# Attention maxima with a pace of their own, retention steps shifted by one, and the second half's head sums taken early

## The chip, the cores and the metric

The kernel runs on one core of a Trainium2 chip. Five engines work side by side, each on its own queue in program order: TensorE (PE: matmuls and transposes, its weight loads shown apart as PEld), VectorE (DVE), ScalarE (ACT), GpSimd (POOL) and SyncE (SP), which here only issues DMAs. The metric is the device time of one execution in microseconds. Before the change it is 2969.17 us, the median of three runs (2965.57 to 2970.82).

## The reference, cut to what matters

A decoder block over 2048 tokens of width 1024, all in float32:

```python
h = rms_norm(x, attn_norm_w)
r_q, r_k, r_v, r_g, c_q, c_kv, k_pe = split(h @ w_in)
y_ret = retention_group(r_q, r_k, r_v, r_g, ...)  # 8 heads of 64: causal scores with decay,
                                                  # a state carried over chunks, group norm, silu gate
y_mla = mla_group(c_q, c_kv, k_pe, ...)           # 8 heads: causal softmax attention, low-rank q and kv
x = x + concat(y_ret, y_mla) @ w_out
x = x + conv_ffn(rms_norm(x, ffn_norm_w))         # 1024 -> 2*2816, causal conv of width 3, silu gate, -> 1024
return rms_norm(x, final_norm_w)
```

The causal softmax is `p = softmax(where(key <= query, s, -big))`. The row maximum that is taken off before the exponential must see the masked scores; any shift that is the same for a row gives the same result.

## The kernel before

Matmul operands that carry float32 are split into a high part (rounded copy) and a low part (the difference): `split` (L60 to L68) makes the high part on ACT (L64) or DVE and the low part on POOL or DVE (L68), and `mm3` (L72 to L74) issues three matmuls per product. So nearly every matmul waits for an ACT copy and a POOL or DVE subtraction, and a product is ready only when its low part is.

The program runs in stages. First the input projections that attention needs. Then `side_by_side` runs two generators against each other: `ret_stream` (retention, 16 chunk pairs of 256 tokens for two pairs of heads) and `att_stream` (attention, 8 heads of 4 groups of 512 queries). Each generator yields the cost of the step that it has just written, and the order of the instructions follows from these costs. The compiler's scheduler then fixes each engine's order from the written order and the waits.

A retention chunk (`ret_chunk`) has 16 steps: eight projection steps, and eight that split q and k (tile S), transpose S on PE (L619), form and mask the scores (tile x), multiply with V, update the state, and norm and gate (L682 to L693). The last eight run beside the eight projection steps of the next chunk, one to one. An attention group (`att_group`) has 4g+5 steps: scores (PE, tile s; L759 to L764), exponentials on ACT and their low parts on DVE (tile pc, L768), and the products with v (tile o). Before a group can start, `att_max` must have found the row maxima of its queries: for each of the 4 blocks of 128 queries and each chunk of 512 keys one score matmul into the PSUM tile sm (L727), for the chunk on the diagonal a second matmul that adds the mask (L730: identity `unit` times `mqk`, 256 columns), and a reduction on DVE (L731). sm has one buffer, so the next L727 waits for the L731 before it. The maxima of the next group are spread over the steps of the current one: 4g'+6 units over 4g+5 steps.

Then `out_stream` puts the first eight tokens' tiles (128 tokens each) through the output projection, and `half_0_forms` adds the retention part of the output projection for tiles 8 to 15 (the transposes of the token forms are at L955) and prepares the first half's up-projection operands F (low parts: POOL, L68). `up` (L1087 on) is the up-projection of a half with its conv (L1135 to L1138) and gate; `down` the down-projection and the final norm. Between the halves `half_1_forms` adds the attention heads' part of the output projection for tiles 8 to 15: `att_load` brings the two halves of a head sum (mixa_s) and the softmax denominators' reciprocals (rden_s), POOL adds and scales them (L851, L852), the operands are split, PE multiplies, DVE adds to the residual (L868), ACT squares (L1039), DVE takes the root in ten small instructions (L102 to L114) and scales (L1042), and PE transposes the result for the up-projection.

Of the kernel before, what the change touches and what calls it, by code (L numbers as in the profile page):

```python
# [46 lines left out]
AHEAD = 2  # L47
RET_SHARE = .91
# [5 lines left out]
class Block:  # L54
# [388 lines left out]
    def att_pools(self, ctx):  # L443
        nc, a, tc = self.nc, self.a, self.tc
        self.kp = ctx.enter_context(tc.tile_pool(name="ak", bufs=5, side="right"))
# [8 lines left out]
        m = b1.tile([P, 640], F32R, name="mqk")  # L454
        r = self.raw.tile([P, D], F32, name="raw")[:, :640]
        nc.sync.dma_start(r, a["mask_att"])
        nc.scalar.activation(m, r, AF.Copy)
        self.mkq, self.mqk = m[:, 0:384], m[:, 256:640]
# [3 lines left out]
        self.vts = [b1.tile([P, 4, 160], F32R, name=f"v{i}") for i in range(5)]  # L462
# [54 lines left out]
    def ret_stream(self):  # L517
        nc, a = self.nc, self.a
        hs, pend = {}, None
# [29 lines left out]
        for c in pend:  # L549
            yield c  # L550

    def att_stream(self):
        groups = [(h, g) for h in range(H) for g in range(4)]
        q = None
        for c, q in self.att_max(*groups[0]):
            yield c
        for n, (h, g) in enumerate(groups):
            nxt = self.att_max(*groups[n + 1]) if n + 1 < len(groups) else iter(())
            steps, units = 4 * g + 5, 4 * groups[n + 1][1] + 6 if n + 1 < len(groups) else 0
            owed, qn = 0.0, None  # L560
            for c in self.att_group(h, g, q):
                owed += units / steps
                while owed >= 1:
                    owed -= 1
                    m = next(nxt, None)
                    if m:
                        c += m[0]
                        qn = m[1]
                yield c
            for m in nxt:  # L570
                qn = m[1]
                yield m[0]
            q = qn
# [3 lines left out]
    def ret_chunk(self, p, ch, W, hs):  # L577
        nc, c1, c2, px = self.nc, self.r1, self.r2, self.pr_x
        mm = nc.tensor.matmul
        qk = c2.tile([P, 2, 4, 64], F32, name="qk")  # L580
        vg = c2.tile([P, 2, 256], F32, name="vg")
        V = c2.tile([P, 2, 2, 2, 64], F32R, name="V")
        sg = c2.tile([P, 2, P], F32, name="sg")
# [64 lines left out]
        o = c2.tile([P, 4, 64], F32, name="o")  # L648
# [32 lines left out]
        sq = c1.tile([P, 4, 64], F32, name="gsq")  # L681
# [31 lines left out]
    def att_max(self, h, g):  # L713

        nc, b2 = self.nc, self.b2
        q = b2.tile([98, 2, 512], F32R, name="q")
# [3 lines left out]
        mx = b2.tile([P, 4, 4], F32, name="mx")  # L720
        for i in range(4):
            for c in range(g + 1):
# [4 lines left out]
                nc.tensor.matmul(ps[:, :N], lhsT=q[0:96, 0, i * P:(i + 1) * P], rhs=k[0:96, 0, :N], start=True, stop=c < g)  # L727
# [116 lines left out]
    def att_load(self, t, r, rd, m):  # L844

# [5 lines left out]
        nc.gpsimd.tensor_tensor(r[:, 0], r[:, 0], r[:, 1], op=ALU.add)  # L851
        nc.gpsimd.tensor_tensor(r[:, 0], r[:, 0], rd, op=ALU.mult)  # L852
# [124 lines left out]
    def half_0_forms(self):  # L977
# [3 lines left out]
        def rows(i):  # L981
            for j in range(2):
                nc.sync.dma_start(hn[2 * (i % 2) + j], self.hn_s[4 * j + i])
        for t in (8, 9):
            self.z0_load(t)
        rows(0)
        rows(1)
        for i in range(4):
            self.token_forms(i, hn[2 * (i % 2)], hn[2 * (i % 2) + 1])
# [4 lines left out]
            for t in (8 + 2 * i, 9 + 2 * i):  # L994
                m, y = self.ms[t % 2].rearrange("p (a k x) -> p a k x", a=2, k=4), self.ys[t % 2]
                pss = [self.bank() for _ in range(2)]
                for kc in range(4):
                    self.out_mm(pss, m, kc, kc == 0, kc == 3)
                self.out_add(y, pss)
                nc.sync.dma_start(self.y_s[t], y)  # L1000
                if t + 2 < NT:
                    self.z0_load(t + 2)
# [7 lines left out]
    def z1_load(self, n, r=None):  # L1010
        t = Z1_ORDER[n]
        r = (self.raws[n % 2] if r is None else r).rearrange("p (a k x) -> p a k x", a=2, k=4)
        self.att_load(t, r, self.p1.rearrange("p (k x) -> p k x", k=4), self.ms[n % 2].rearrange("p (a k x) -> p a k x", a=2, k=4))

    def z1_early(self, n):

        if n == 2 * NFB - 3:
            self.nc.sync.dma_start(self.u2.rearrange("p a b -> p (a b)"), self.a["ffn_norm_w"].broadcast_to([P, D]))
            self.ms = self.slots(1)
        if n >= 2 * NFB - 2:  # L1020
            k = n - (2 * NFB - 2)
            self.z1_load(k, self.u.rearrange("p a b -> p (a b)")[:, k * D:(k + 1) * D])

    def half_1_forms(self):

        nc, hn, fnw = self.nc, self.fs, self.u2.rearrange("p a b -> p (a b)")
        for n in range(2):
            nc.sync.dma_start(self.ys[n], self.y_s[Z1_ORDER[n]])
        self.pay()
# [368 lines left out]
```

## Time and profile before

| | before |
|---|---|
| median of 3 runs | 2969.17 us |
| profiled execution | 2968.21 us (span 2966.4 us, 1.8 us around it) |
| PE busy | 2768.4 us (93%) |
| DVE busy | 1953.1 us (66%) |
| ACT busy | 1348.3 us (45%) |
| POOL busy | 1957.8 us (66%) |
| retention and attention side by side | 270 to 1290 us |
| half_0_forms | 1423 to 1484 us |
| up, down of the first half | 1484 to 1922, 1922 to 2179 us |
| half_1_forms | 2179 to 2282 us |
| up, down of the second half | 2282 to 2700, 2700 to 2966 us |

Busy time of PE is modelled (matmuls are pipelined, their durations overlap), so the step from the start of one to the start of the next counts, and so do the idle times before an instruction together with what ended them. PEclk is the clock that was granted to TensorE, as a share of its upper level, 2.4 GHz; 0.5 is the lower one, 1.2 GHz.

### The profile page before, as it was taken

The page shows a single profiled execution, that of the slowest core. Times are in us where ns is not written, and L with a number is a line of the kernel's source. Part 1 is how long each engine was busy: PE and PEld are TensorE (multiplying, and loading weights), DVE is VectorE, ACT ScalarE, POOL GpSimd, SP SyncE. Part 2 cuts the span into 40 slices and gives each one's busy share as a digit, 9 for nine tenths or more (in the row PEclk, how much of TensorE's full clock was granted, in tenths as well). Part 3 has the DMA queues.
Part 4 walks back from the last instruction along what each step waited for, and adds up shares of the span by engine and source line. Part 5 has one row for each costly group of instructions (what it writes and reads, how often), then busy time and mean ns, then how long its engine had stood idle before and what let it go on. Part 6 is the DMA issues. An engine that isn't in the chain of part 4 may idle for free.

```text
span 2966.4 us, 37611 instructions
## 1 busy us (share of the span) xinstructions
PE 2768.4 (93%) x12800; PEld 2237.1 (75%) x12800; DVE 1953.1 (66%) x3265; ACT 1348.3 (45%) x2544; POOL 1957.8 (66%) x1478
## 2 busy tenths in 40 slices
PE   7998999988999999989899999989995999999998
PEld 6976777777777777767787777778874888887887
DVE  8765676667666666754458888844266888887243
ACT  5435656555655555551333333333334433333343
POOL 2035656566655556663599999765558999995564
PEclk9999999999999999999899999989997999999999
DMA  7663112223211121326622222264552222224453
GB/s 259 219 209 95 53 55 65 59 70 97 63 54 55 54 65 45 97 88 196 241 94 77 73 85 81 79 228 153 187 192 96 71 79 86 79 74 163 149 193 109
DMA packets 153360, 332.91 MB, mean 112 GB/s; under 512 B 35016, under 2 KB 68296, under 8 KB 147024
## 3 DMA queue, kind: packets, MB, share of 16 engines
q1 hardware_dynamic: 153168, 330.51, 34.1%
q8 instruction: 101, 1.65, 0.2%
q14 instruction: 91, 0.75, 0.1%
HBM read 237.71 MB, written 92.75 MB: 111 GB/s over the span
## 4 chain that ended last, share of the span: by engine, by line
PE 56%; DVE 15%; ACT 7%; issue 6%; POOL 6%; DMA 3%; SPq 0%; POOLq 0%; ACTq 0%; DVEq 0%
PE b L74 10%; PE b L73 10%; PE b L72 10%; PE pm L74 3%; PE pm L72 3%; PE pm L73 3%; DVE w L1137 2%; DVE u L1131 2%; DVE w L1138 2%; PE sm L727 2%; ACT w L1136 2%; PE s L759 2%; PE x L661 2%; DVE w L1163 2%; PE s L764 1%
## 5 line engine op out<-in xcount | busy, mean ns | idle before, releaser
L68 POOL TENSOR_TENSOR w<-raw,w 128x512 fp32r<-128x512 f32 (+2 forms) x315 | 523.2, 1676 | 256.2 <-ACT w L64 243.8
L74 PE MATMUL b<-F,w 128*128 128x512 f32 x1232 | 492.5, 400 | 0.0
L72 PE MATMUL b<-F,w 128*128 128x512 f32 x1232 | 487.7, 396 | 3.8 <-DVE u L1131 3.8
L73 PE MATMUL b<-F,w 128*128 128x512 f32 x1232 | 487.5, 396 | 3.1 <-POOL F L68 3.1
L777 POOL TENSOR_TENSOR den<-den,pc 128x512 f32<-128x512 f32 (+2 forms) x256 | 294.1, 1149 | 207.8 <-ACT pc L766 189.8
L64 ACT ACTIVATE w<-raw 128x512 fp32r<-128x512 f32 (+2 forms) x328 | 214.4, 658 | 348.1 <-PE b L74 179.0
L72 PE MATMUL b<-w 128*128 128x512 f32 x832 | 330.2, 397 | 21.0 <-DVE u L1131 13.0
L74 PE MATMUL b<-w 128*128 128x512 f32 x832 | 328.1, 394 | 1.6 <-POOL w L68 1.5
L73 PE MATMUL b<-w 128*128 128x512 f32 x832 | 328.0, 394 | 0.0
L731 DVE TENSOR_REDUCE mx<-sm 128x1 f32<-128x512 f32 (+2 forms) x320 | 194.1, 607 | 173.8 <-PE sm L727 126.9
L68 DVE TENSOR_TENSOR w<-xr,w 128x512 fp32r<-128x512 f32 x88 | 110.4, 1255 | 284.9 <-ACT w L64 284.9
L72 PEld LDWEIGHTS b<-F,w 128*128 128x128 f32 x1232 | 232.6, 189 | 65.7 <-DVE u L1131 11.0
L73 PEld LDWEIGHTS b<-F,w 128*128 128x128 f32 x1232 | 232.5, 189 | 62.4 <-POOL F L68 3.5
L74 PEld LDWEIGHTS b<-F,w 128*128 128x128 f32 x1232 | 232.4, 189 | 54.5
L768 DVE TENSOR_TENSOR pc<-s,pc 128x512 fp32r<-128x512 f32 (+1 forms) x320 | 197.6, 619 | 99.6 <-ACT s L767 74.6
L1136 ACT ACTIVATE w<-u,cw 128x1024 f32<-128x1024 f32 x88 | 109.5, 1244 | 333.1 <-DVE u L1131 198.5
L1137 DVE SCALAR_TENSOR_TENSOR w<-u,cw,w 128x1024 f32<-128x1024 f32 x88 | 165.7, 1883 | 128.7 <-ACT w L1136 128.7
L766 ACT ACTIVATE pc<-s 128x512 fp32r<-128x512 f32 (+1 forms) x320 | 172.6, 539 | 148.5 <-PE s L764 142.1
L72 PE MATMUL pm<-w,h 128*128 128x512 f32 x512 | 211.1, 412 | 6.3 <-DVE t L598 4.8
L68 POOL TENSOR_TENSOR w<-xr,w 128x512 fp32r<-128x512 f32 x110 | 204.6, 1872 | 9.4 <-ACT w L64 9.4
L74 PE MATMUL pm<-w,h 128*128 128x512 f32 x512 | 206.5, 403 | 0.0
L73 PE MATMUL pm<-w,h 128*128 128x512 f32 x512 | 205.7, 402 | 0.0
(263 smaller groups left out, 6618.6 us busy)
## 6 DMA issues: line engine op xcount, KB each, us to landing
raw<-in_w_down SPq DMA_DIRECT2D x88, 512.0 KB
h<-hT_s SPq DMA_DIRECT2D x32, 1024.0 KB
xr<-in_w_up SPq DMA_DIRECT2D x44, 512.0 KB
raw<-in_w_up SPq DMA_DIRECT2D x44, 512.0 KB
g_s<-w SPq DMA_DIRECT2D x44, 512.0 KB
xr<-g_s SPq DMA_DIRECT2D x88, 256.0 KB
hT_s<-hT SPq DMA_DIRECT2D x16, 1024.0 KB
raw<-in_w_ret SPq DMA_DIRECT2D x16, 512.0 KB
```

Of the source, the lines that this page charges most:

```text
L64: nc.scalar.activation(hi, src, AF.Copy)
L68: eng.tensor_tensor(lo, src, f32(hi), op=ALU.subtract)
L72: mm(out, lhsT=lh, rhs=rh, start=start, stop=False)
L73: mm(out, lhsT=lh, rhs=rl, start=False, stop=False)
L74: mm(out, lhsT=ll, rhs=rh, start=False, stop=stop)
L661: mm(ps[:, x * P:x * P + 256], lhsT=l, rhs=r, start=n == 0, stop=n == len(ops) - 1)
L731: nc.vector.tensor_reduce(mx[:, i, c:c + 1], ps[:, :w], axis=AX, op=ALU.max)
L766: nc.scalar.activation(pc[:, 0, r0:], ps[:, r0:], AF.Exp, scale=ATT_SCALE)
L768: nc.vector.tensor_tensor(pc[:, 1, r0:], ps[:, r0:], f32(pc[:, 0, r0:]), op=ALU.subtract)
L777: nc.gpsimd.tensor_tensor(den[:, r0:], den[:, r0:], hi[:, r0:], op=ALU.add)
L1136: nc.scalar.activation(acc, x[:, 2:1026], AF.Identity, scale=w2, bias=b)
L1137: nc.vector.scalar_tensor_tensor(acc, x[:, 1:1025], w1, acc, op0=ALU.mult, op1=ALU.add)
```

## The change

The maxima of a group come from a generator of their own that may run two groups ahead and gives 1.1 units per attention step, whatever the group. The mask of the diagonal chunk is added on DVE in the pass that takes the maximum (one instruction with two results, from a mask that lies in SBUF in float32) and no longer by a matmul. A retention chunk's last eight steps begin one step later, and the eighth runs in the chunk after the next. Some retention tiles have one buffer for two; q and the maxima have three. `half_0_forms` puts tiles 8 and 9 ahead of the first token forms. The head sums of tiles 8 to 15 are loaded, added, scaled and written to a scratch `mixn_s` during the first down-projection, one head tile in four blocks, and `half_1_forms` only loads and splits them; its norms are taken a tile behind. In the last block of `up` the conv of the values is written after that of the gates.

```diff
     def ret_stream(self):
@@
-                    for _ in range(8):
+                    for n in range(8):
                         yield next(it)
-                        if pend is not None:
+                        if n and pend is not None:
                             yield next(pend, 0)
+                        if n == 2 and old is not None:
+                            yield next(old, 0)
@@
-                    if pend is not None:
-                        for c in pend:
-                            yield c
-                    pend = it
+                    old, pend = pend, it
     def att_stream(self):
@@
+        def maxima():
+            for n, hg in enumerate(groups):
+                while n > self.at + 2:
+                    yield 0
+                for c, qs[n] in self.att_max(*hg):
+                    yield c
+                done.add(n)
+        self.at, mx, owed = 0, maxima(), 0.0
         for n, (h, g) in enumerate(groups):
-            nxt = self.att_max(*groups[n + 1]) if n + 1 < len(groups) else iter(())
-            steps, units = 4 * g + 5, 4 * groups[n + 1][1] + 6 if n + 1 < len(groups) else 0
@@
-            for c in self.att_group(h, g, q):
-                owed += units / steps
+            self.at = n
+            while n not in done:
+                yield next(mx)
+            for c in self.att_group(h, g, qs.pop(n)):
+                owed = min(owed + MAX_PACE, 2.0)
                 while owed >= 1:
                     owed -= 1
-                    m = next(nxt, None)
+                    c += next(mx, 0)
@@
     def ret_chunk(self, p, ch, W, hs):
-        qk = c2.tile([P, 2, 4, 64], F32, name="qk")
+        qk = c1.tile([P, 2, 4, 64], F32, name="qk")
...
     def att_max(self, h, g):
@@
                 if c == g:
-                    m = self.mqk[:, 0:256] if w > P else self.mqk[:, P:384]
-                    nc.tensor.matmul(ps[:, N - 256:N], lhsT=self.unit, rhs=m, start=False, stop=True)
-                nc.vector.tensor_reduce(mx[:, i, c:c + 1], ps[:, :w], axis=AX, op=ALU.max)
+                    nc.vector.tensor_tensor_reduce(ps[:, :w], ps[:, :w], self.mqk[:, 512 - w:], scale=1.0, scalar=-3.0e38, op0=ALU.add, op1=ALU.max, accum_out=mx[:, i, c:c + 1])
+                else:
+                    nc.vector.tensor_reduce(mx[:, i, c:c + 1], ps[:, :w], axis=AX, op=ALU.max)
@@ half_0_forms
+        tile_out(8)
         for i in range(4):
+            if i:
+                tile_out(9 + 2 * i - 1)
+            tile_out(9 + 2 * i) if i < 3 else None
             self.token_forms(i, hn[2 * (i % 2)], hn[2 * (i % 2) + 1])
@@
-            for t in (8 + 2 * i, 9 + 2 * i):
...
+        tile_out(15)
         self.up_start(0)
@@
+    def heads_load(self, n):
+        t = Z1_ORDER[n]
...
+        self.heads_in(t, self.hr, self.hd)
+
+    def heads_store(self, n):
+        self.heads_sum(self.hr, self.hd)
+        self.nc.sync.dma_start(self.mixn_s[n], self.hr[:, 0])
@@ z1_early
+        if n % 4 == 2 and n < 4 * TH:
+            self.heads_load(n // 4)
+        if n % 4 == 1 and 4 < n < 4 * TH + 4:
+            self.heads_store(n // 4 - 1)
@@ half_1_forms
+            if n:
+                scaled(n - 1)
             self.out_add(y, pss)
-            h, ss = hn[n % 4], self.cs.tile([P, 1], F32, name="ss")
-            nc.scalar.activation(h, y, AF.Square, scale=D ** -0.5, accum_out=ss)
-            nc.sync.dma_start(self.y_s[t], y)
-            r = self.rstd(self.cs, ss, "n")
-            nc.vector.scalar_tensor_tensor(h, y, r, fnw, op0=ALU.mult, op1=ALU.mult)
...
@@ up
-            conv(av, fb, 1)
+            if fb < NFB - 1:
+                conv(av, fb, 1)
             add(u[:, 0, 514:], product(fb, 3), u2)
             add(u[:, 0, 2:514], product(fb, 5), p1)
             conv(ag, fb, 0)
+            if fb == NFB - 1:
+                conv(av, fb, 1)
```

Three places show how the instructions move. In the changed kernel the line numbers are a little higher: mm3 is at L73 to L75, split's subtraction at L69, the maxima at L732 to L736, the transposes of the token forms at L966.

PE before, in a group of attention: the diagonal chunk's score matmul into sm is followed by the mask matmul L730 (w, h are retention's projection operands, x its scores, s attention's scores).

```order
L764 MATMUL s_4004<-q_3500,k_3510 128x384
L72 MATMUL pm_3887<-w_2224,h_3566 128x512
L727 MATMUL sm_3984<-k_3979,q_3966 128x256
L730 MATMUL sm_3984<-mqk_2435,unit_2433 128x256
L73 MATMUL pm_3887<-w_2224,h_3566 128x512
L74 MATMUL pm_3887<-w_2224,h_3566 128x512
L636 MATMUL x_3996<-Qs_3990,K_3989 128x256
L635 MATMUL x_3996<-Q_3988,K_3989 128x256
L636 MATMUL x_3996<-Qs_3990,K_3989 128x256
L788 MATMUL sm_4015<-pc_3949,ones_2439 2x512 x2
```

PE after the change, at a like place: after the diagonal L732 (256 columns, sm_4073) no mask matmul stands, and the next one into sm (sm_4103) comes after other work.

```order
L666 MATMUL x_4112<-Rst_4107,Q_3979 128x256
L666 MATMUL x_4112<-Rst_4107,Qs_3981 128x256
L666 MATMUL x_4112<-V_3553,SC_3986 128x256
L732 MATMUL sm_4073<-k_4068,q_4024 128x256
L764 MATMUL s_4122<-q_3447,k_3457 128x256
L765 MATMUL s_4122<-q_3447,k_3457 128x256
L768 MATMUL s_4122<-mkq_2436,unit_2434 128x256
L666 MATMUL x_4112<-V_3553,SC_3986 128x256
L666 MATMUL x_4112<-Rst_4107,Q_3979 128x256
L732 MATMUL sm_4103<-k_3457,q_4024 128x512
```

DVE before, in the maxima of one group (mx): every chunk has one reduction.

```order
L768 TENSOR_TENSOR pc_2599<-s_2594,pc_2599 128x256
L731 TENSOR_REDUCE mx_2537<-sm_2606 128x1
L768 TENSOR_TENSOR pc_2638<-s_2633,pc_2638 128x256
L662 TENSOR_REDUCE o_3004<-x_3068 128x128
L731 TENSOR_REDUCE mx_2537<-sm_2609 128x1
L731 TENSOR_REDUCE mx_2537<-sm_2645 128x1
L684 TENSOR_REDUCE gs2_3154<-gsq_3152 128x4
```

DVE after the change: a diagonal chunk has two rows, the pass over sm and mqk and a one-column row for its second result.

```order
L734 ISA sm_2808,mx_2701<-sm_2808,mqk_2440 128x256
L734 ISA mx_2701 128x1
L605 TENSOR_TENSOR qk_2833<-t1_3154,t2_3155 128x256
L612 SCALAR_TENSOR_TENSOR sg_2836<-th_3226,vg_2834 128x256
L773 TENSOR_TENSOR pc_2849<-s_2844,pc_2849 128x512
L736 TENSOR_REDUCE mx_2701<-sm_2856 128x1
L773 TENSOR_TENSOR pc_2870<-s_2865,pc_2870 128x384
L736 TENSOR_REDUCE mx_2701<-sm_2877 128x1
```

So PE loses one matmul for each of the 128 diagonal chunks, and DVE has one small row more for each.

PE before, at the start of `half_0_forms`: the last output projection of tile 7 (tile u, weights w, operand m) is followed by the transposes L955 of the first token forms, which read the normed rows w_14903.

```order
L73 MATMUL u_14801<-w_13521,m_14741 128x512
L74 MATMUL u_14801<-w_13521,m_14741 128x512
L72 MATMUL u_14802<-w_13521,m_14741 128x512
L73 MATMUL u_14802<-w_13521,m_14741 128x512
L74 MATMUL u_14802<-w_13521,m_14741 128x512
L955 MATMUL b_14917<-ident_73,w_14903 128x128 x4
L955 MATMUL b_14922<-ident_73,w_14903 128x128 x4
L955 MATMUL b_14927<-ident_73,w_14903 128x128 x4
L955 MATMUL b_14932<-ident_73,w_14903 128x128 x4
L72 MATMUL b_14961<-w_13866,w_14901 128x512
L73 MATMUL b_14961<-w_13866,w_14901 128x512
```

PE after the change: the products of tile 9 (b_14828, b_14829; tile 8's 24 stand ahead of them) come before those transposes (L966, w_14781).

```order
L74 MATMUL b_14828<-w_13742,w_14779 128x512
L75 MATMUL b_14828<-w_13742,w_14779 128x512
L73 MATMUL b_14829<-w_13742,w_14779 128x512
L74 MATMUL b_14829<-w_13742,w_14779 128x512
L75 MATMUL b_14829<-w_13742,w_14779 128x512
L966 MATMUL b_14861<-ident_74,w_14781 128x128 x4
L966 MATMUL b_14866<-ident_74,w_14781 128x128 x4
L966 MATMUL b_14871<-ident_74,w_14781 128x128 x4
L966 MATMUL b_14876<-ident_74,w_14781 128x128 x4
L73 MATMUL b_14905<-w_13727,w_14779 128x512
L74 MATMUL b_14905<-w_13727,w_14779 128x512
```

So 48 matmuls that need only retention's outputs and weights now stand between tile 7 and the transposes.

POOL before, in `half_1_forms`: splits (L68) of the head operands w alternate with the adding and scaling of the heads (L851, L852); F is the up-projection's operand.

```order
L851 TENSOR_TENSOR raw_14892<-raw_14892 128x512
L852 TENSOR_TENSOR raw_14892<-raw_14892,p1_14889 128x512
L68 TENSOR_TENSOR w_19718<-raw_14892,w_19718 128x512
L851 TENSOR_TENSOR raw_14893<-raw_14893 128x512
L852 TENSOR_TENSOR raw_14893<-raw_14893,p1_14889 128x512
L68 TENSOR_TENSOR w_19718<-raw_14893,w_19718 128x512
L851 TENSOR_TENSOR raw_14892<-raw_14892 128x512
L68 TENSOR_TENSOR F_19870<-u_14887,F_19870 128x4x128 x4
L852 TENSOR_TENSOR raw_14892<-raw_14892,p1_14889 128x512
L68 TENSOR_TENSOR w_19718<-raw_14892,w_19718 128x512
```

POOL after the change, at the same place: the splits alone are left.

```order
L69 TENSOR_TENSOR w_19644<-raw_14770,w_19644 128x512
L69 TENSOR_TENSOR w_19644<-raw_14771,w_19644 128x512
L69 TENSOR_TENSOR w_19644<-raw_14770,w_19644 128x512
L69 TENSOR_TENSOR w_19644<-raw_14771,w_19644 128x512
L69 TENSOR_TENSOR F_19788<-u_14765,F_19788 128x4x128 x4
L69 TENSOR_TENSOR w_19644<-raw_14770,w_19644 128x512
L69 TENSOR_TENSOR w_19644<-raw_14771,w_19644 128x512
L69 TENSOR_TENSOR F_19788<-u_14765,F_19788 128x4x128 x4
```

The adds and scalings of the eight tiles (now L858 and L859) stand in the first down-projection instead, the first add as early as the end of `half_0_forms`' loads.

## Rows read from the trace of the kernel before

**Rows 1.** The profile page: span, and busy time of PE.

```profile
span 2966.4 us, 37611 instructions
PE 2768.4 (93%) x12800; PEld 2237.1 (75%) x12800; DVE 1953.1 (66%) x3265; ACT 1348.3 (45%) x2544; POOL 1957.8 (66%) x1478
```

**Rows 2.** Windows by stage: stretch, length, busy per engine, granted clock, DMA share, GB/s.

```profile
270.00:1290.00 1020.00, 944.42 (x4799) 756.35 (x4797) 689.95 (x1494) 602.76 (x1256) 610.89 (x609) 0.97 0.22 65
1423.00:1484.00 61.00, 53.01 (x258) 45.11 (x258) 33.65 (x59) 25.85 (x45) 34.90 (x28) 0.92 0.73 256
...
1922.00:2179.00 257.00, 246.26 (x1061) 201.48 (x1060) 96.83 (x116) 93.40 (x170) 154.64 (x107) 0.97 0.55 183
2179.00:2282.00 103.00, 64.60 (x273) 50.68 (x271) 85.00 (x168) 42.59 (x82) 74.91 (x56) 0.80 0.46 160
```

**Rows 3.** Waits of PE, 270 to 1290 us: total, times, longest.

```profile
PE sm L727 <- DVE mx L731: 21.9, 19, 2.4
PE x L619 <- POOL S L68: 15.6, 16, 1.6
PE sm L788 <- DVE mx L731: 9.2, 3, 3.4
```

**Rows 4.** Mask matmuls among PE's groups by form, 270 to 1290 us: busy, mean ns.

```profile
L730 PE MATMUL sm<-mqk,unit 128*128 128x256 f32 x120 | 34.7, 289 | 0.0
```

**Rows 5.** Timeline of PE around one mask matmul: start, duration.

```profile
607.22 0.28 PE L730 MATMUL sm<-mqk,unit 128*128 128x256 f32 x1
607.34 0.41 PE L661 MATMUL x<-V,SC 128*128 128x256 f32 x2
```

**Rows 6.** DVE's groups by form, 270 to 1290 us: busy, mean ns, idle before.

```profile
L731 DVE TENSOR_REDUCE mx<-sm 128x1 f32<-128x512 f32 x217 | 148.9, 686 | 129.8 <-PE sm L727 124.9 <-PE sm L730 3.8
...
L686 DVE TENSOR_TENSOR o<-o,sg 128x256 f32<-128x256 f32 x29 | 36.9, 1273 | 0.0
...
L637 DVE TENSOR_TENSOR x<-x,mask 128x256 f32<-128x256 f32 x58 | 24.7, 426 | 11.8 <-PE x L636 11.6
...
L731 DVE TENSOR_REDUCE mx<-sm 128x1 f32<-128x256 f32 x30 | 12.7, 422 | 20.3 <-PE sm L730 20.0
```

**Rows 7.** Timeline of PE at the start of half_0_forms.

```profile
1422.66 0.39 PE L74 MATMUL u<-w,m 128*128 128x512 f32 x1
1431.04 3.65 PE L955 MATMUL b<-ident,w 128*128 128x128 f32 x16 [7.99 <-DMA w<-hn_s]
1434.34 0.78 PE L72 MATMUL b<-w 128*128 128x512 f32 x1
```

**Rows 8.** Timeline of POOL, start and end of half_0_forms.

```profile
1419.72 2.53 POOL L68 TENSOR_TENSOR w<-raw,w 128x512 fp32r<-128x512 f32 x2 [6.61 <-ACT w L64]
...
1480.78 1.31 POOL L68 TENSOR_TENSOR w<-xr,w 128x512 fp32r<-128x512 f32 x1 [0.35 <-ACT w L64]
```

**Rows 9.** Waits of PE, 1915 to 1960 us (end of up, start of down).

```profile
PE b L72 <- DVE u L1131: 10.4, 4, 4.6
```

**Rows 10.** Waits of PE, 2179 to 2290 us.

```profile
PE b L955 <- DVE w L1042: 26.9, 4, 11.4
PE b L72 <- ACT w L64: 7.6, 3, 4.3
PE b L73 <- POOL F L68: 3.1, 1, 3.1
```

**Rows 11.** Waits of POOL in the same stretch.

```profile
POOL raw L852 <- DMA p<-rden_s: 14.7, 3, 7.8
```

**Rows 12.** Timeline of POOL, 2243 to 2290 us.

```profile
2244.62 1.28 POOL L1092 TENSOR_TENSOR w<-xr 128x512 f32<-128x512 f32 x1 [0.91 <-PE b L955]
...
2280.28 2.49 POOL L68 TENSOR_TENSOR F<-u,F 128x512 fp32r<-128x512 f32 x2
2282.72 1.28 POOL L68 TENSOR_TENSOR w<-raw,w 128x512 fp32r<-128x512 f32 x1
2283.95 2.52 POOL L68 TENSOR_TENSOR F<-u,F 128x512 fp32r<-128x512 f32 x2
```

**Rows 13.** Timeline of DVE, two of the ten small steps of a root.

```profile
2219.40 1.20 DVE L113 SCALAR_TENSOR_TENSOR z_n<-z_n 128x1 f32<-128x1 f32 x1
...
2227.26 0.15 DVE L105 TENSOR_SCALAR r_n<-v_n 128x1 int32<-128x1 int32 x1
```

More of the change, by code (lines that the diff above doesn't have):

```diff
@@ L47 @@
 AHEAD = 2
+MAX_PACE = 1.1
 RET_SHARE = .91
@@ L444, in att_pools @@
         nc, a, tc = self.nc, self.a, self.tc
-        self.kp = ctx.enter_context(tc.tile_pool(name="ak", bufs=5, side="right"))
+        self.kp = ctx.enter_context(tc.tile_pool(name="ak", bufs=6, side="right"))
         self.b1 = b1 = ctx.enter_context(tc.tile_pool(name="a1", bufs=1, side="right"))
@@ L453, in att_pools @@
         nc.scalar.activation(self.unit, self.ident, AF.Copy)
-        m = b1.tile([P, 640], F32R, name="mqk")
-        r = self.raw.tile([P, D], F32, name="raw")[:, :640]
-        nc.sync.dma_start(r, a["mask_att"])
+        m = b1.tile([P, 384], F32R, name="mkq")
+        r = self.raw.tile([P, D], F32, name="raw")[:, :384]
+        nc.sync.dma_start(r, a["mask_att"][:, 0:384])
         nc.scalar.activation(m, r, AF.Copy)
-        self.mkq, self.mqk = m[:, 0:384], m[:, 256:640]
+        self.mkq = m[:, 0:384]
+        self.mqk = b1.tile([P, 512], F32, name="mqk")
+        nc.gpsimd.memset(self.mqk, 0.0)
+        nc.sync.dma_start(self.mqk[:, 384:512], a["mask_att"][:, 384:512])
         self.ones = b1.tile([P, 2], F32R, name="ones")
         nc.vector.memset(f32(self.ones), 1.0)
-        self.vts = [b1.tile([P, 4, 160], F32R, name=f"v{i}") for i in range(5)]
+        self.vts = [b1.tile([P, 4, 160], F32R, name=f"v{i}") for i in range(6)]
         for v in self.vts:
@@ L647, in ret_chunk @@
             rst = Rst.rearrange("p h a d -> p (h a d)")
-        o = c2.tile([P, 4, 64], F32, name="o")
+        o = c1.tile([P, 4, 64], F32, name="o")
         for ib in range(2):
@@ L715, in att_max @@
         nc, b2 = self.nc, self.b2
-        q = b2.tile([98, 2, 512], F32R, name="q")
+        q = self.b3.tile([98, 2, 512], F32R, name="q")
         r = self.raw.tile([P, D], F32, name="raw")
@@ L719, in att_max @@
         self.split(q[0:96, 0], q[0:96, 1], r[0:96, 0:512])
-        mx = b2.tile([P, 4, 4], F32, name="mx")
+        mx = self.b3.tile([P, 4, 4], F32, name="mx")
         for i in range(4):
@@ L983, in rows, with tile_out @@
                 nc.sync.dma_start(hn[2 * (i % 2) + j], self.hn_s[4 * j + i])
+        def tile_out(t):
+            m, y = self.ms[t % 2].rearrange("p (a k x) -> p a k x", a=2, k=4), self.ys[t % 2]
+            pss = [self.bank() for _ in range(2)]
+            for kc in range(4):
+                self.out_mm(pss, m, kc, kc == 0, kc == 3)
+            self.out_add(y, pss)
+            nc.sync.dma_start(self.y_s[t], y)
+            if t + 2 < NT:
+                self.z0_load(t + 2)
         for t in (8, 9):
@@ L1049, in half_1_forms @@
         self.up_start(1, 1)
+        scaled(TH - 1)
         self.token_forms(2, hn[0], hn[1])
@@ L1245, in down @@
                 prepare(n + 2)
-                if half == 0 and q:
-                    if NFB - 6 <= fb < NFB - 2:
+                if half == 0:
+                    if q and NFB - 6 <= fb < NFB - 2:
                         self.out_weights_att(fb - NFB + 10)
@@ L1261, in down @@
                 prepare((q + 1) * NFB + 1)
-                if half == 0 and q:
-                    self.z1_early(2 * NFB - 1)
+                if half == 0:
+                    self.z1_early((q + 1) * NFB - 1)
                 for t in range(4):
@@ L1278, in run @@
         self.y_s = dp.tile([NT, P, D], F32, name="y_s")
+        self.mixn_s = dp.tile([TH, P, 4, P], F32, name="mixn_s")
         self.hn_s = dp.tile([TH, P, D], F32, name="hn_s")
```

71 lines of the change are left out of this document (33 added, 38 removed).

## The prediction

> **What bounds the kernel now.** I read the page's busy times first, then the windows by stage, then PE's waits inside the stages that the change touches, and last the timelines at the two transitions. PE is busy for 2768 of 2966 us, no other engine for more than two thirds [rows 1]. So the kernel is bound by PE, and a change can win in three ways only: fewer matmuls, fewer idle stretches of PE, or a higher granted clock. The windows tell where the second and third lie [rows 2]. Side by side, retention and attention take 1020 us with PE busy for 944, so 76 us idle, at a granted clock of 0.97; 3% of 1020 us is some 31 us of clock at the most. `half_0_forms` leaves 8 of 61 us idle at 0.92, `half_1_forms` 38 of 103 us at 0.80, and the first `down` 11 of 257. The other stages are not touched.
>
> **Part 1, the mask on DVE.** 128 mask matmuls go. One is shown as 0.28 to 0.29 us long [rows 4], but it overlaps its neighbours: the next matmul starts 0.12 us after it [rows 5]. 128 x 0.12 = 15.4 us of PE; as PE is idle for 7% of this stage, some of that falls on time that PE would have waited anyway: I count 14.
>
> DVE pays. No instruction before adds and takes a maximum in one pass, so I bound it. A maximum alone takes 422 ns for 256 columns; a multiplication of a PSUM tile with a mask in SBUF, result back into PSUM, which is the nearest row, takes 426 [rows 6]. I take the pass as long as the maximum that it replaces, and add the one-column row that the order shows behind it, at the 0.15 us of a small DVE step that nothing disturbs [rows 13]: 128 x 0.15 = 19 us. DVE is busy for 690 of 1020 us, so this mostly lies beside other work. But sm has one buffer, and PE's score matmul queues behind the maximum. I charge a third: +6 us. The ends: 0 if the read hides wholly; and for a dear pass the dearest row of this stage, a multiplication with two SBUF inputs at 1273 ns for 256 columns [rows 6], which is the slower rival below.
>
> **Part 2, retention a step later.** PE waits for POOL's low part of S before the transposes of a chunk, 16 times, 15.6 us [rows 3], the longest 1.6 us. In the order of before, a median of 10,240 columns of matmul stand between the last projection of a chunk and its first transpose, in the changed one 15,360. The added 5,120 are ten 512-column matmuls, about 2.3 us (the 0.12 us of 256 columns, twice, ten times). This is more than the longest of these waits, so they should go. PE then reaches the next wait sooner, so I count three quarters: -12 us (ends 0 and -15.6). The single buffers cost nothing by the written order: each of the tiles is read for the last time by an earlier step than the one that writes it anew.
>
> **Part 3, the pace.** PE waits for DVE's maxima for 21.9 us at L727 and 9.2 us at L788, 31 us in all [rows 3]. These are the places where one maximum follows the other too closely, since 4g'+6 units over 4g+5 steps give two per step in a group g = 0 (10 over 5) and a third of one in g = 3 (6 over 17). In the order of before 178 of 319 neighbouring maxima have fewer than 4,096 columns of matmul between them, in the changed one 109, so 39% fewer. 39% of 31 us is 12; I count -10, as 74 of them still stand under 3,072 columns (100 before). The ends are 0 and -31. The granted clock of this stage I leave where it is; regaining all of it would be another 31 us. Stage sum: -14 + 6 - 12 - 10 = -30 us.
>
> **Part 4, half_0_forms.** PE has nothing for 7.99 us, from the last matmul of tile 7 to the first transposes, which wait for the normed rows from DRAM; the transposes then stand 3.30 us before the next matmul starts [rows 7]. Now 48 matmuls come first: at about 0.23 us each 11 us of work, more than the gap. Their operand is ready: POOL's low part of tile 8 ends at 1419.72 + 2.53 = 1422.25 us, before the gap starts [rows 8]. The gap goes, and the transposes may start at the higher clock. At the other end POOL's work for the up-projection reaches into 1482 us [rows 8], so `up` may not start a full 8 us sooner without waiting for it. I count -8 (ends -10 and -3).
>
> **Part 5, the conv order.** The gaps of 10.4 us around the end of `up` wait for DVE's adds [rows 9]. The order of DVE and ACT there reads the same in both kernels: the scheduler had put the values' conv where its inputs are ready, and puts it there still. Price 0.
>
> **Part 6, the head sums.** Eight tiles' loads (512 KB and twice 128 KB), a store of 256 KB and two POOL instructions each move into the first `down`. There POOL is busy for 155 of 257 us and DMA for 0.55 [rows 2], and PE's 11 idle us there are nearly all the 10.4 at its very start [rows 9]. The added 16 POOL instructions are some 21 us at 1.3 us each, the length of one of 512 columns [rows 12]. Price 0, at most +5 if a weight's low part comes late in the queue behind them.
>
> **Part 7, half_1_forms.** PE waits 26.9 us for DVE's scaled rows (L1042), 7.6 for head operands and 3.1 for the F low part [rows 10]. POOL itself stands 14.7 us for rden_s [rows 11]. That wait goes, the 7.6 us behind it as well, and POOL has two instructions fewer per tile. What is late next is not PE: it is POOL's row of 30 instructions for the first up-projection operands, from 2244.62 us nearly without a gap to the end of the F low parts at 2286.47 us [rows 12]. This row keeps its length of 42 us, and it begins when the transposes of the third token forms are there. With the norms a tile behind and no wait for rden_s, I work out that this start comes about 6 us sooner, so -6. The bottom is -3. The top is -20: DVE's small steps take 1.20 us where one is disturbed and 0.15 where not [rows 13], and with POOL relieved more of them may be short.
>
> The Trainium skill ("SBUF — State Buffer", Who interferes with whom) says that a DVE instruction with two SBUF inputs contends with a GpSimd instruction that reads SBUF, and one with at most one does not. The rows agree in kind: 1273 ns for two SBUF inputs, 426 for one from PSUM, both 256 columns [rows 6]. By that rule the new pass, with its scores in PSUM, is undisturbed, and its price is the one taken above; that speaks against the slower rival.
>
> **Sum.** -30 - 8 + 0 + 0 - 6 = -44 us against the profiled 2968.2 us gives 2924. The median stands 1 us above that execution: 2925 us.
>
> **Rivals.**
> (a) The pacing and the shift gain nothing: PE merely reaches the next wait of a dense net of waits. For it: a maximum's round trip stays, sm keeps its one buffer, and the 149 us of 512-column maxima alone [rows 6] stay on DVE. Against it: the added distance exceeds the longest wait. Then -14 + 6 - 8 - 3 = -19: 2950 us.
> (b) More than the sum: evenly spaced waits keep the granted clock up, and `half_1_forms` gains its upper end. Half of the 31 us of clock, all of the S wait and 20 us of `half_1_forms`: -14 + 6 - 15 - 12 - 15 - 8 - 20 = -78: 2891 us.
> (c) Slower: the pass on DVE becomes the wait. Diagonal chunks are 320 columns wide in the mean. At 1273 / 256 = 4.97 ns per column that is 1.59 us instead of some 0.5, so 1.1 x 128 = 140 us more of DVE, which would then be busy for some 830 of 1020 us, with each pass holding the only sm. If half of it is exposed, +70 in place of the +6: -50 + 70 = +20: 2989 us. It decides from 50 / 64 = 0.8 us more per pass on. For it: the instruction does not occur before, and has a second result. Against it: the PSUM-with-mask row.
> (d) The changed parts do what they say, but the loads of the heads and the POOL work put there stall the first `down`, and the one-buffer tiles of retention tie its steps together, so that the gains are eaten: about 2967.
>
> **Chances.** The forecast 0.55, (a) 0.18, (b) 0.13, (c) 0.09, (d) 0.05. The likeliest case alone reaches from 2908 to 2941. The range that leaves out half of (b), (c) and (d) is 2893 to 2958. Within 0.2% (6 us, about what a measurement of this kernel can tell from no change): 0.05. Faster 0.86, slower 0.09.
>
> **What would show it.** In the changed profile: no mask matmul into sm; the new pass at about 0.43 us for 256 columns with a read of 0.15 (right), or above 1.2 us (c). PE's wait for S below 4 us and for maxima near 20 us; the stage ends near 1260 us. No wait of PE at the first transposes of `half_0_forms`, and 8 us off that stage. The four gaps at the end of `up` unchanged at some 10 us. No wait of PE in the first `down` behind its start. In `half_1_forms` no wait for rden_s, but waits for scaled rows still, and the F low part still the last to come. The forecast is wrong if the stage of retention and attention gains less than 15 us or more than 50.

## The result, and the profile after

The changed kernel takes 2932.49 us (median of four, 2932.01 to 2944.54), before 2969.99 in the same comparison: a ratio of 0.9889 (95% interval 0.9874 to 0.9903), 33 us faster by the ratio, 37 by the medians. Forecast were 2925. Its profiled execution took 2932.35 us, 35.9 less than the one before.

The page answers to [rows 1] with:

```profile
span 2930.6 us, 37521 instructions
PE 2735.2 (93%) x12672; PEld 2218.0 (76%) x12672; DVE 1966.6 (67%) x3393; ACT 1346.3 (46%) x2544; POOL 1956.2 (67%) x1480
```

128 matmuls are gone and DVE has 128 instructions more. PE's share stays at 93%: the kernel is as bound by PE as before. Where the time went is read from PE's starts at places that both programs have:

| place | before | after | gain so far |
|---|---|---|---|
| first output projection of the first half (tile u) | 1315.74 | 1279.79 | 36.0 |
| last matmul of tile 7 | 1422.66 | 1386.13 | 36.5 |
| start of the first up (first product with F) | 1483.95 | 1446.80 | 37.2 |
| its last product | 1923.04 | 1891.74 | 31.3 |
| start of the second up | 2274.59 | 2236.76 | 37.8 |
| last matmul | 2957.89 | 2921.36 | 36.5 |

So attention and retention gave 36 us (forecast 30), `half_0_forms` 0.6 (forecast 8), the first up lost 5.9 (forecast 0), and the first down with `half_1_forms` gave 6.5 (forecast 6). The windows of the stages, columns as in [rows 2]:

```profile
270.00:1279.80 1009.80, 934.67 (x4773) 755.85 (x4773) 722.59 (x1650) 617.44 (x1288) 629.31 (x622) 0.98 0.22 66
1386.00:1447.00 61.00, 54.37 (x260) 44.45 (x259) 32.65 (x56) 22.27 (x39) 30.74 (x26) 0.94 0.80 287
1892.00:2141.00 249.00, 235.55 (x1009) 191.12 (x1008) 88.30 (x107) 88.52 (x161) 157.76 (x111) 0.97 0.63 206
2141.00:2237.00 96.00, 66.81 (x307) 55.72 (x306) 85.62 (x172) 41.86 (x83) 55.48 (x42) 0.83 0.42 151
```

In the first stage PE still waits, but for something else. Its waits from 270 to 1280 us, answering to [rows 3]:

```profile
PE sm L732 <- DVE mx L736: 18.1, 17, 5.0
PE sm L745 <- DVE n L69: 16.1, 10, 2.7
PE sm L732 <- ACT otl L795: 6.6, 10, 1.0
...
PE sm L732 <- DVE mx L734: 3.2, 5, 1.0
...
PE x L624 <- POOL S L69: 1.9, 1, 1.9
```

The wait for the low part of S (15.6 us) is down to 1.9. The waits for maxima (L736 and L734) fell from 31 to 21. New is a wait of PE for DVE's row of maxima (tile n, split for the transposes at L745): 16 us. Before, it was 3:

```profile
PE sm L740 <- DVE n L68: 3.2, 7, 0.7
```

All waits together are 74 us against 78 up to the same matmul (1315.7 us before). The new pass itself, DVE's groups by form (answering to [rows 6]):

```profile
L734 DVE CUSTOM_DVE_ANT_0 sm<-sm,mqk 128x512 f32<-128x512 f32 x32 | 22.2, 695 | 9.5 <-PE sm L732 9.3
L734 DVE DVE_READ_ACCUMULATOR2_ANT mx<- 128x1 f32 x128 | 18.0, 141 | 0.0
...
L734 DVE CUSTOM_DVE_ANT_0 sm<-sm,mqk 128x256 f32<-128x256 f32 x32 | 13.7, 429 | 3.8 <-PE sm L732 3.2
```

It takes 429 ns for 256 columns where the plain maximum took 422, and its read 141 ns.

At `half_0_forms` the 8 us gap is gone and the first transposes take 1.91 us in place of 3.65, but waits stand where none stood, 6.7 us in all (PE's timeline, answering to [rows 7]):

```profile
1387.39 0.47 PE L73 MATMUL b<-w 128*128 128x512 f32 x1 [0.88 <-DVE y L879]
...
1398.37 1.91 PE L966 MATMUL b<-ident,w 128*128 128x128 f32 x16
...
1407.64 0.50 PE L75 MATMUL b<-w 128*128 128x512 f32 x1 [1.42 <-POOL w L69]
...
1418.14 0.79 PE L73 MATMUL b<-w 128*128 128x512 f32 x1 [3.48 <-ACT w L65]
```

In `half_1_forms` (2141 to 2252 us, answering to [rows 10]) the waits for head operands (ACT w, 7.6 us) are gone, those for scaled rows and for F are not:

```profile
PE b L966 <- DVE w L1067: 25.3, 3, 13.9
PE b L74 <- POOL F L69: 5.0, 1, 5.0
```

### The profile page after: what moved, and what is told of

Its sections match the earlier page's. It is cut to its first block, busy times and chain, and to the rows that moved or that the text cites. A ratio compares the mean times of both kernels' runs of the same rounds, so it can differ in the third digit from the quotient of the medians.

```text
span 2930.6 us, 37521 instructions
## 1 busy us (share of the span) xinstructions
PE 2735.2 (93%) x12672; PEld 2218.0 (76%) x12672; DVE 1966.6 (67%) x3393; ACT 1346.3 (46%) x2544; POOL 1956.2 (67%) x1480
## 4 chain that ended last, share of the span: by engine, by line
PE 35%; DVE 13%; issue 5%; ACT 4%; POOL 4%; DMA 3%; SPq 0%; ACTq 0%; DVEq 0%; POOLq 0%
PE b L73 10%; PE b L75 10%; PE b L74 10%; DVE w L1174 2%; DVE u L1168 2%; DVE w L1175 2%; ACT w L1173 2%; DVE w L1204 2%; POOL w L69 1%; DMA raw<-mixa_s 1%; DMA w<-rden_s 1%; DVE w L1203 1%; ACT u L1202 1%; POOL F L69 1%; PE x L666 1%
## 5 line engine op out<-in xcount | busy, mean ns | idle before, releaser
L69 POOL TENSOR_TENSOR w<-raw,w 128x512 fp32r<-128x512 f32 (+2 forms) x315 | 522.6, 1674 | 236.9 <-ACT w L65 214.5
L73 PE MATMUL b<-F,w 128*128 128x512 f32 x1232 | 492.4, 400 | 6.2 <-DVE u L1168 6.2
L75 PE MATMUL b<-F,w 128*128 128x512 f32 x1232 | 489.0, 397 | 1.1 <-POOL w L69 1.1
L73 PE MATMUL b<-w 128*128 128x512 f32 x832 | 330.1, 397 | 17.6 <-DVE u L1168 13.0
L75 PE MATMUL b<-w 128*128 128x512 f32 x832 | 327.9, 394 | 2.3 <-POOL w L69 2.3
L69 DVE TENSOR_TENSOR w<-xr,w 128x512 fp32r<-128x512 f32 x88 | 107.8, 1225 | 292.5 <-ACT w L65 282.7
L73 PEld LDWEIGHTS b<-F,w 128*128 128x128 f32 x1232 | 232.5, 189 | 67.6 <-DVE u L1168 13.8
L75 PEld LDWEIGHTS b<-F,w 128*128 128x128 f32 x1232 | 232.4, 189 | 59.9 <-POOL w L69 2.0
L1174 DVE SCALAR_TENSOR_TENSOR w<-u,cw,w 128x1024 f32<-128x1024 f32 x88 | 166.6, 1893 | 133.8 <-ACT w L1173 133.8
L73 PE MATMUL pm<-w,h 128*128 128x512 f32 x512 | 209.3, 409 | 11.2 <-DVE t L603 3.2
L69 POOL TENSOR_TENSOR w<-xr,w 128x512 fp32r<-128x512 f32 x110 | 204.5, 1871 | 12.1 <-ACT w L65 12.1
L74 PE MATMUL pm<-w,h 128*128 128x512 f32 x512 | 203.5, 398 | 0.0
L75 PE MATMUL pm<-w,h 128*128 128x512 f32 x512 | 203.2, 397 | 0.0
L73 PEld LDWEIGHTS b<-w 128*128 128x128 f32 x832 | 158.7, 191 | 54.8 <-DVE u L1168 16.7
```

Source lines behind the costliest of these rows:

```text
L69: eng.tensor_tensor(lo, src, f32(hi), op=ALU.subtract)
L73: mm(out, lhsT=lh, rhs=rh, start=start, stop=False)
L74: mm(out, lhsT=lh, rhs=rl, start=False, stop=False)
L75: mm(out, lhsT=ll, rhs=rh, start=False, stop=stop)
L1174: nc.vector.scalar_tensor_tensor(acc, x[:, 1:1025], w1, acc, op0=ALU.mult, op1=ALU.add)
```

## The experiments

All ratios are to the kernel before, run in turn on the same chip; after (the changed kernel) stands at 0.9889. The medians of before in the four comparisons lie between 2966 and 2970 us, so a difference of a few microseconds between two comparisons says little. Profiles are of one execution each.

**The mask.** `pe_mask` puts the matmul back into the changed kernel; `mask_only` gives the kernel before nothing but the new pass.

```diff
 pe_mask, against after
+  if c == g: nc.tensor.matmul(ps[:, N - 256:N], lhsT=self.unit, rhs=m, start=False, stop=True)
-  nc.vector.tensor_tensor_reduce(ps[:, :w], ps[:, :w], self.mqk[:, 512 - w:], ...)
+  nc.vector.tensor_reduce(mx[:, i, c:c + 1], ps[:, :w], axis=AX, op=ALU.max)
 mask_only, against before: the reverse
```

> The changed kernel with the mask back on PE (128 matmuls of 256 columns, a plain maximum on DVE), all else kept. Theory A (the columns counted): PE gets 128 x 0.12 = 15 us back and some clock is lost with it, so about 2948 us (2944 to 2955). Rival (PE would have waited there anyway, and DVE loses its 128 reads of 0.14 us): 2930 to 2937 us.

> The kernel before with the mask added on DVE in the pass that takes the maximum, nothing else. Theory C (PE's columns: what putting the mask back cost the changed kernel): 5 to 10 us faster than before, about 2959 us. Rival (with the old pace two maxima follow each other in a step, and the mask matmul lies on that round trip, so it is worth more there; the changed kernel with the old pace was 23 us faster than shift alone): 15 to 25 us faster, about 2946 us.

`pe_mask` took 2937.52 us, ratio 0.99 (0.9886 to 0.9915): some 3 to 5 us slower than after, which its interval does not tell from nothing; it lies just above the rival's span and clear below theory A. `mask_only` took 2958.84, ratio 0.9969 (0.9956 to 0.9983): 9 to 10 us faster than before. Its stage is 7.9 us shorter, while PE's waits in it rose from 78 to 86 us: half of the 15.4 us of columns came back as waiting. That is the size that the sum had (-14 and +6), but not its place. The +6 was charged for PE's scores that queue behind DVE at the one sm buffer, and the waits for maxima did not rise: 29 us in `mask_only`, 31 before. Other waits grew. Those of `mask_only` in the stage (270 to 1307.8 us):

```profile
PE x L622 <- POOL S L68: 18.1, 17, 2.5
PE sm L730 <- DVE mx L734: 17.3, 18, 2.5
PE s L762 <- DVE pc L771: 13.1, 11, 5.7
PE sm L791 <- DVE mx L734: 9.8, 5, 2.5
...
PE sm L743 <- DVE n L68: 5.3, 9, 1.7
...
PE sm L730 <- DVE mx L732: 1.5, 2, 0.8
```

Before, up to the same matmul, the wait for S is 15.9 us, that for the row 3.2, and that for the exponentials' low parts:

```profile
PE s L759 <- DVE pc L768: 9.7, 9, 3.5
```

**The shift.** `no_shift` undoes it, `shift_only` is the kernel before with it alone.

```diff
 no_shift, against after (shift_only, against before: the reverse)
-  if n and pend is not None:
+  if pend is not None:
       yield next(pend, 0)
-  if n == 2 and old is not None:
-      yield next(old, 0)
```

> The changed kernel with retention's last eight steps beside the next chunk's eight steps again, as before the change; all else kept. Theory A (the shift took PE's wait for the low part of S, 15.6 us before and none in this stage after): the wait returns and the time rises by 8 to 15 us, about 2943 us. Rival (PE only reached the next wait sooner, the gain is elsewhere): 2930 to 2936 us, with the wait for S back and others smaller by as much.

> The kernel before with retention's last eight steps begun one step later, nothing else. Theory B (the shift carries the stage's gain, and the new pace takes some of it back: with the old pace the stage was 52 us shorter than before, of which the mask is some 8): 35 to 45 us faster than before, about 2927 us. Rival (the shift is worth the 22 us that undoing it cost, whatever the pace): about 2945 us.

`no_shift` took 2954.43, ratio 0.9963 (0.995 to 0.9976), 22 us slower than after; `shift_only` 2946.05, ratio 0.9934 (0.9922 to 0.9947), 20 us faster than before. Of `no_shift` neither line holds (2943, and 2930 to 2936); of `shift_only` the rival's 2945 was right. The profiled executions are the longest of either (2963.69 and 2949.34 us). PE's waits in the stage, first of `no_shift`, then of `shift_only`:

```profile
PE x L622 <- POOL S L69: 19.4, 25, 2.3
```

```profile
PE sm L727 <- DVE mx L731: 18.6, 19, 2.8
PE sm L740 <- DVE n L68: 8.9, 14, 1.5
PE s L759 <- ACT q L741: 8.8, 7, 2.1
...
PE x L619 <- POOL S L68: 2.5, 2, 1.5
```

With the shift the wait for S is nearly gone (15.9 to 2.5 us). The waits for maxima fall by 12 us too (31 to 19), others rise by as much (that for the row from 3 to 9), so that all waits fall by 13, from 78 to 65 us. The clock of the stage goes from 0.97 to 0.98, and PE's busy time there, for the same matmuls, from 966 to 958 us: the shift gives back more than the wait that it removes.

**The pace.** `old_pace` ties the maxima of a group to the steps of the one before again, `pace_only` is the kernel before with the new generator and all the buffers of the changed kernel, the single ones of retention included.

```diff
 old_pace, against after
-  owed = min(owed + MAX_PACE, 2.0)
+  owed += units / steps        # 4g'+6 units over 4g+5 steps
 pace_only, against before: the reverse, with the buffers of after
```

> The changed kernel with the maxima of the next group spread over the current group's steps again; all else kept. Theory A (the even pace took idle time and above all gave back the clock, 0.97 to 0.99 in this stage): 10 to 25 us slower, about 2950 us, clock of the stage back to 0.97. Rival (the pace only turned waits for a maximum into waits for the row of maxima, 3 to 18 us): 2930 to 2937 us.

> The kernel before with the maxima in a generator of their own at 1.1 per step, two groups ahead, with the buffers of the changed kernel (six for k and v, three for q and the maxima, one for the retention tiles), nothing else. Theory B (the even pace by itself brings waits for the row of maxima): 5 to 20 us slower than before, 2972 to 2987 us. Rival (the pace helps alone, and only collides with the shifted retention): 5 to 25 us faster, 2942 to 2962 us.

`old_pace` took 2919.38, ratio 0.984 (0.9827 to 0.9853): 13 us faster than after. `pace_only` took 2961.75, ratio 0.9979 (0.9969 to 0.9989), 4 to 6 us faster than before (its profiled execution, 2955.67 us, is the shortest of eleven): PE's waits in its stage rose from 78 to 84 us, and the clock from 0.97 to 0.99. Neither line on `old_pace` holds; on `pace_only` the rival does, at its edge. The waits of `old_pace` in the stage (270 to 1264 us) sum to 47 us, not 74:

```profile
PE s L763 <- DVE pc L772: 9.9, 7, 5.0
PE sm L731 <- DVE mx L735: 9.1, 14, 2.0
PE pm L73 <- DVE t L602: 8.1, 7, 1.4
PE sm L744 <- DVE n L69: 6.8, 12, 1.0
```

So beside the shift and the new mask, the even pace costs. The candidate was the new wait for the row of maxima. `late_rows` gives it one step more (the other line lets a generator that has ended give 0):

```diff
 late_rows, against after
             while n not in done:
-                yield next(mx)
+                yield next(mx, 0)
@@
         self.split(n2[:, :, 0], n2[:, :, 1], nm, "dve", "dve")
         yield 1, q
+        yield 1, q
         row = self.pa_m.tile([P, 512], F32, name="sm")
```

> The changed kernel with one step more between DVE's row of maxima and the transposes that PE makes of it. Theory D (with the new pace these transposes come too soon, and this wait of 18 us is what the pace costs): the wait falls below 6 us, and the time by 8 to 12 us, to about 2922 us. Rival (the pace's cost is spread over all uses of the one sm buffer): the wait falls, others grow, 2929 to 2936 us.

2919.98 us, ratio 0.9834 (0.9815 to 0.9852): 12.5 us faster than after, and as fast as `old_pace`. Its waits (270 to 1261 us, 57 us in all):

```profile
PE s L765 <- DVE pc L774: 14.2, 8, 3.8
PE sm L732 <- DVE mx L736: 13.4, 16, 2.6
...
PE sm L746 <- DVE n L69: 3.0, 6, 0.9
```

The wait for the row went from 16 to 3 us, and the time fell by nearly as much. That is what the new pace costs. Which rows wait can be read from the traces one by one, for the groups g = 0 of heads 1 to 7. With the old pace their six units lay over 17 steps: before and in `old_pace` 23,424 to 25,984 columns of matmul stand between the last score into sm and the transposes, and PE waits for none of these seven rows. With the new pace 6,144 to 11,264 columns stand there, and six of the seven wait, 12.1 us together. In `late_rows` it is 10,752 to 14,848 columns and 0.6 us. One such group, first in after, then in `old_pace`:

```profile
455.55 0.50 PE L732 MATMUL sm<-k,q 96*128 96x512 f32 x1 [0.61 <-DVE mx L734]
...
460.57 0.60 PE L745 MATMUL sm<-ident,n 128*2 128x128 f32 x4 [1.73 <-DVE n L69]
```

```profile
469.60 0.40 PE L731 MATMUL sm<-k,q 96*128 96x512 f32 x1
...
485.27 0.60 PE L744 MATMUL sm<-ident,n 128*2 128x128 f32 x4
```

In after DVE needs 3.7 to 6.3 us in these seven groups from the end of the last maximum to the end of the split: other work stands in its queue between, and some single instructions are long. In this one the last two are:

```profile
458.04 1.26 DVE L67 CAST n<-nm 128x4 fp32r<-128x4 f32 x1
459.33 1.18 DVE L69 TENSOR_TENSOR n<-nm,n 128x4 fp32r<-128x4 f32 x1
```

In `old_pace` the same two take 0.16 us each. `late_rows` also changes the pace a little: its groups have 4g+7 units, 52 for a head, and 1.1 for each of the head's 44 steps gives 48, so that its maxima lag. No run parts the two; that the gain is the row's is read from the waits that fell. With this mended, the even pace is worth as much as the old one, no more.

**half_0_forms.** `old_half0` has the old order there; `old_pace_half0` the old pace as well; `old_bufs` is that kernel with the buffers of before for k, v, q and the maxima; `one_ahead` (on `old_pace`) puts one tile ahead of the first token forms, four behind the third, and keeps one pair of buffers for the head sums.

```diff
 old_half0, against after
-  tile_out(8)
   for i in range(4):
-      if i: tile_out(9 + 2 * i - 1)
-      tile_out(9 + 2 * i) if i < 3 else None
       self.token_forms(i, ...)
+      for t in (8 + 2 * i, 9 + 2 * i): tile_out(t)
 old_bufs: k 6 -> 5, v 6 -> 5, q 3 -> 2, mx 3 -> 2
 one_ahead, against old_pace: tile 8; forms 0; 9; forms 1; 10, 11; forms 2; 12, 13; forms 3; 14, 15
-  self.hr, self.hd = fs[n % 2], fs[2 + n % 2]
+  self.hr, self.hd = fs[0], fs[2]
```

> The changed kernel with half_0_forms in the order of before (tiles 8 and 9 behind the first token forms); all else kept. Theory A (the 8 us gap went, but only two tiles stand behind the third token forms, in whose shadow POOL makes the first weights, so up began without them): the gap of 8 us returns, up is some 6 us shorter, the time falls to about 2927 us (2924 to 2932). Rival (the gap was worth its 8 us, and what up lost comes from the head sum's add that now stands in POOL's queue): 2937 to 2941 us.

> The changed kernel with both the old pace of the maxima and the old order of half_0_forms. If the two act apart (13 and 3 us): about 2916 us (2912 to 2919). If the order of half_0_forms only mattered through what the stage before left behind: 2919 to 2925 us.

> The changed kernel with the old pace and the old order of half_0_forms (2913 us), and with the buffers of before for k and v (5) and for q and the maxima (2). Theory (the buffers only serve maxima that run two groups ahead): 2910 to 2918 us. Rival (the third q buffer is what took the wait for q's row, 8.8 us in the kernel with the shift alone and 1.4 here): 2920 to 2930 us.

> The changed kernel with the old pace, one tile (8) and no more ahead of the first token forms in half_0_forms, four tiles behind the third as before, and the head sums in one pair of buffers that up uses, so that none is loaded before the first down-projection. Theory A (what half_0_forms lost was the shadow behind the third token forms): part of the 8 us gap is filled and nothing lost in up, 2907 to 2911 us. Rival (the loads of the normed rows set this stage, whatever PE does meanwhile): 2912 to 2916 us.

`old_half0`: 2929.22, ratio 0.9874 (0.9861 to 0.9887), 3 us under after, inside the noise and inside theory A's span. Its profile says what the totals can't: `half_0_forms` takes 60.8 us, as long as after's 60.7, with the gap of 7.73 us back; the first up is 5.0 us shorter. The reason is on POOL. The first instruction for the weights' forms, of `old_half0` and of after:

```profile
1423.16 1.32 POOL L1124 TENSOR_TENSOR w<-xr 128x512 f32<-128x512 f32 x1
```

```profile
1433.05 1.31 POOL L1129 TENSOR_TENSOR w<-xr 128x512 f32<-128x512 f32 x1 [3.79 <-PE b L966]
...
1443.08 1.31 POOL L858 TENSOR_TENSOR w<-w 128x512 f32<-128x512 f32 x1
```

In after it waits for PE's transposes of the third token forms, which the change put behind two more tiles; up starts at 1446.5 and 1446.8, so in after POOL has 14 us for the first weights and in `old_half0` 23. PE then has 7.3 us of waits in this up, 4.4 in `old_half0`, and in its first 65 us a clock of 0.97 instead of 1.00. The head sum's add that crept in here (L858) is in both, so it is not the cause of the difference. The other traces agree: with the new order the first up takes 444 to 445 us (`late_heads` too, which has no such add), with four tiles behind the third forms 439 to 440 (`one_ahead` too, which has a tile ahead of the first). `old_pace_half0` took 2912.94, ratio 0.9825 (0.9812 to 0.9839): within the noise the two undone parts add up. `old_bufs` took 2909.37, ratio 0.9799 (0.9777 to 0.982), the fastest by its median, though not told from `old_pace_half0`: with the old pace the added buffers are not needed.

`one_ahead` took 2932.49, ratio 0.9872 (0.985 to 0.9894), 13 us slower than `old_pace` and outside both spans. Up to the end of the first up it is 4.1 us ahead of `old_pace`, the 5 us of the order again and nothing for the gap; from there to the second up it loses 20. With one pair of buffers, the load of a head waits for the store of the one before, and POOL, which takes its instructions in order, stands for it with the weights' splits behind. In the 145 us from 1925 on PE then waits 14 us, 10.7 of them for POOL's low parts, where `old_pace` has 2.7 in all, and the clock is 0.93 and 0.95 in its two parts (1925 to 2000, 2000 to 2070), there 1.00. POOL's group for the first add (1893 to 2032 us), of `one_ahead` and of `old_pace`:

```profile
L857 POOL TENSOR_TENSOR w<-w 128x512 f32<-128x512 f32 x7 | 9.0, 1283 | 34.0 <-DMA w<-mixa_s 24.1 <-DMA xr<-g_s 5.6 <-DMA w<-rden_s 4.3
```

```profile
L857 POOL TENSOR_TENSOR w<-w 128x512 f32<-128x512 f32 x6 | 7.8, 1302 | 8.2 <-issue 4.5 <-DMA w<-mixa_s 3.7
```

**The heads.** `late_heads` has the loads, adds and norms of before in `half_1_forms`.

```diff
 late_heads, against after: z1_load, z1_early and half_1_forms of before
-  self.nc.sync.dma_start(r, self.mixn_s[n])
+  self.att_load(t, r, self.p1..., self.ms[n % 2]...)
```

> The changed kernel with the heads of tiles 8 to 15 added in half_1_forms again and its norms in place, all else kept. Theory (the 6 us that half_1_forms lost are these): about 2938 us, with POOL's wait for rden_s back at 10 us or more. Rival (POOL's row for the first weights sets the end whatever stands before it): 2930 to 2934 us.

2940.01 us, ratio 0.991 (0.9895 to 0.9925), 7.5 us slower by the medians, though the intervals touch. From the last product of the first up to the start of the second it takes 351.5 us, after 345.0, before 351.6: the theory holds. POOL's waits in its `half_1_forms` are the ones of [rows 11] again:

```profile
POOL raw L859 <- DMA p<-rden_s: 13.7, 3, 6.5
```

## Why the prediction was right or wrong

The total was right (37 us for 44, inside the range), but not every term, and that it fits is in part luck. In the stage of retention and attention 36 us came for 30, as the sum of a shift that gave more than counted, a pace that cost instead of giving, and a gain of mask and shift together that no term had.

**Part 1, the mask: right in size, -8.** Alone it gave 9 to 10 us; in the changed kernel, undone, 3 to 5, which is not told from nothing. The price of the pass (429 and 141 ns, forecast 422 and 150) came from the right row, and the slower rival (c) fell with it. The +6 was right in size only: it did not come at sm, where the waits fell by 2 us, but at other waits.

**Part 2, the shift: right, too small.** -12 was counted, 20 to 22 measured, alone and when undone. The wait for S vanished as worked out, and all waits together fell by 13 us, so the term holds for the waits. What it left out is the clock: PE's busy time for the same matmuls fell by 8 us. That PE reaches the next wait sooner is half true: the waits for maxima fell along with S, others rose.

**Part 3, the pace: wrong.** The step that failed is "39% fewer" close neighbours, so 10 us less waiting. It counted the distance from one maximum to the next, and not from a group's last maximum to the transposes of its row. There DVE has more to do than one reduction, and the old pace had kept just the rows of the groups g = 0 far from it. The waits for maxima did fall by 10 us, but with the old pace they fall by 21 (`old_pace`), and the pace alone takes off 3 (`pace_only`), so not even that was the pace's; and 13 us of new wait came at L745. `late_rows` takes these away, and 12.5 us of time with them. What the pace does give, the clock of `pace_only`, was named and left out of the sum, and the shift gives it too.

**Part 4, half_0_forms: wrong, +5 for -8.** The gap went as forecast, yet the stage stayed as long. That `up` might have to wait was named, and priced at nothing to speak of: the sum took POOL's end at 1482 us as fixed and did not look at what POOL's chain starts from, the transposes of the third forms, and how many tiles stand behind them. In the stage itself the operands came later: ACT waits 12.0 us there for the loads of retention's rows (raw from mix_s), before not at all, and PE 6.7 us for ACT, POOL and DVE. DMA is busy for 0.80 of the stage (0.73 before). That the fuller PE brought this on was not tried.

**Parts 5 to 7: right.** The waits at the end of up are 10.1 us (10.4 before). The head sums cost the first down little: PE waits 3.2 us for POOL's low parts in it, before not at all, where the forecast had no wait. POOL's row in `half_1_forms` starts at 2205.66 and ends with the F low parts at 2248.65, 43 us, as long as before; counted from the last product of up it begins 7.7 us sooner (forecast 6).

What stays open: with the old pace, mask and shift together gave some 18 us more than the two alone (47 in `old_pace`, 9 to 10 in `mask_only`, 20 in `shift_only`; the parts outside the stage come to nothing there). The waits for maxima fall to 10 us where both are there, from 29 with the mask alone and 19 with the shift alone. That the added buffers do it is excluded by `old_bufs`; that it is the retention tiles' single buffers was not tried.

## What to carry to other kernels

To space out the uses of a single buffer, count the distance behind each kind of use by what the other engine has to do there: the long link is the chain that closes a group (here 3.7 to 6.3 us of DVE where PE waited), not the reductions in it. Before filling a gap with work from further back, look at what that work was hiding: here two tiles of matmuls had covered POOL's first weights. A helper's work is free on an in-order engine only while its operands are there before its turn; a second buffer is what makes it so.

## What the runs showed of the hardware

DVE's pass that adds a mask and takes the maximum, PSUM in place, runs at the rate of the plain maximum: 298, 429, 560 and 695 ns for 128 to 512 columns against 284, 422, 555 and 686, and its second result is an instruction of its own of 141 ns. The granted clock of a stage doesn't follow the sum of PE's waits: in the first stage of one execution each it was 0.97 with 78 us of them (before), 0.99 with 84 (`pace_only`) and 0.99 with 47 (`old_pace`).
